# A two-layer decoder trunk on one core: the next stage's first weights split before the norm into x tiles, later weight work queued behind the norm, the convolution's third product on its own

## The chip, the core and the metric

The kernel runs on one core of one Trainium2 chip. The metric is the device time of one execution in microseconds (us); the time of a kernel is the median of its runs. Engines are called PE (TensorE; PEld its weight loads), DVE (VectorE), ACT (ScalarE), POOL (GpSimd) and SP (SyncE, which only issues DMAs here).

## What is computed

A residual stream of 16 learned meta tokens and 512 input tokens (528 columns), 1024 wide, goes through two layers. Layer 0 is FFN, short gated convolution, FFN; layer 1 is FFN, attention with a forget gate, FFN. Keys, values and gates are computed once between the layers. Everything is in float32.

```python
def swiglu(x, wg, wu, wd):
    return (jax.nn.silu(x @ wg) * (x @ wu)) @ wd

for l in range(DEPTH):                                   # 2
    h = layer_norm(ALPHA * h + 0.5 * swiglu(h, ffn1_wg[l], ffn1_wu[l], ffn1_wd[l]), ...)
    if l < N_A:                                          # layer 0
        mix = short_conv(h, conv_w_in[l], conv_w[l], conv_w_out[l])
    else:                                                # layer 1
        mix = forgetting_attention(h, attn_w_q[j], attn_w_o[j], k_sh, v_sh, c_sh)
    h = layer_norm(ALPHA * h + mix, ...)
    h = layer_norm(ALPHA * h + 0.5 * swiglu(h, ffn2_wg[l], ffn2_wu[l], ffn2_wd[l]), ...)
    if l == N_A - 1:
        k_sh, v_sh, c_sh = shared_kv(h, kv_w, f_bias)
```

`short_conv` projects to three parts (gate b, gate c, value), convolves c times value over three positions, and multiplies by b.

## The kernel before

**Layout.** The stream `y` lies transposed in SBUF: 128 partitions by 8 blocks of the 1024 channels by 528 columns. The columns are worked on in two halves, h = 0 and 1, of 264 columns in layer 0 and 256 in layer 1 (`SPAN`).

**Products.** Every float32 operand is split into a high part, rounded to a narrower format by a cast on ACT, and a low part, the rest, by a subtraction on DVE. A product is three matmuls for each step k: high times low, low times high, high times high (`gemms`, L229). For weights the split is `split_w` (cast L121 into `wh`, subtraction L122 into `wl`), for activations `split_x` (L242 into `xh`, L243 into `xl`). Weights come by DMA from SP into three `raw` buffers of 1 MB and are split into five pairs of tiles `wh`, `wl`; 14 x tiles (`xtile`) hold right operands. `gemms` counts a step (`tick`) after three matmuls; `later(n, fn)` traces `fn` n steps on, which puts `fn`'s matmuls there in PE's queue.

**Order.** The order on PE is that of the program (`manual_schedule`). On the other engines a scheduler orders the instructions when the kernel is built, by readiness in a model and by priority, which follows the program; a norm's operations get a priority 600 higher (`SOON`). Each queue then runs in its order.

**A Mixed stage** (two FFNs of layer 0, keys and values, both FFNs of layer 1) multiplies 256 gate columns and 256 up columns at a time as two-by-two blocks with seven products in place of eight (`Unit`: p1 to p7 with left operands a11, a12, s1 to s4, a22 and right operands b11, b21, t1 to t4, b22). The right operands t1 to t4 are sums of the halves of `y` and are made on DVE in `Mixed.sums`; the left sums s1 to s4 are made in `Quads.sums`. As t1 to t4 need both halves of the columns, the first 256 columns of most stages are a `Direct` unit: plain products, first for half 0 (b11, b21), then for half 1 (b12, b22), 96 matmuls each, with left operands a11, a21, a12, a22. Its a11 goes into x tiles (L557), the others into `wh`, `wl`.

**A boundary.** Five of the six norms sit in a `down` (L463): the product back to 1024 channels, in the order column blocks 0 to 2 of half 0, 0 to 2 of half 1, 3 to 7 of half 0, 3 to 7 of half 1. A product for one block and half is 18 matmuls (6 steps) at the end of an FFN and 24 (8 steps) after convolution or attention. Each block is added to `y` on DVE (L475), squared on ACT (L387) and summed on POOL (L391 `y`, L393 squares). `LAG` steps after the last block of a half, `Norm.post` (L395) puts eight statistics matmuls (L401) on PE. `Norm.finish` follows: v (L411 on ACT, L412 on DVE), eight small operations on DVE (L332 to L340), b (L416), then in pairs of blocks the scaling L420, L421 on DVE, L424 on ACT and `split_x`. Five such boundaries matter here: into the convolution (1), into the second FFN (2), into keys and values (3), into the queries (4) and into the last FFN (5). Boundaries 2, 3 and 5 lead to a `Direct` unit; 1 and 4 to plain products (`Plain`).

**Convolution and queries.** `conv_u` (L719) makes gate c and value (`pcc`, `pcv`) for a block and half, `conv_b` (L734) gate b (`pcb`); from block 2 on, L757 runs all three in lockstep. `project` (L894) runs several heads in lockstep: L1005 three heads of half 0.

Of the kernel before, what the change touches and what calls it, by code (L numbers as in the profile page):

```python
# [35 lines left out]
LAG = (5, 7)  # L36
# [10 lines left out]
def trunk_kernel(  # L47
# [60 lines left out]

    def split_w(src, shape, home=None):
# [12 lines left out]
        nc.vector.tensor_tensor(b, src, a.bitcast(F32), ALU.subtract)  # L122
# [34 lines left out]
    class Quads:  # L157
# [4 lines left out]
        def __init__(self, aps):  # L162
            self.aps, self.raws, self.got, self.home = aps, {}, {}, {}
# [15 lines left out]
        def sums(self):  # L179
            if "s" in self.got:  # L180
                return
            s = wp.tile([P, KD * P], F32, tag="ws", bufs=1, name="s")
            s = s.rearrange("p (j k n) -> p j k n", j=2, k=KH)
            self.got["s"] = s
            a11, a21, a22 = self.part(0, 0), self.part(1, 0), self.part(1, 1)
            nc.vector.tensor_tensor(s, a21, a22, ALU.add)  # L186
            nc.vector.tensor_tensor(a21, a11, a21, ALU.add)
            nc.vector.tensor_tensor(a11, a11, s, ALU.add)

        def __call__(self, name):  # L190
            if name not in self.got:
                if name[0] == "s":
                    self.sums()
                if name == "s4":
                    a12 = self.part(0, 1)
                    nc.vector.tensor_tensor(a12, a12, self.part(0, 0), ALU.add)
# [4 lines left out]
                self.got[name] = split_w(src, (2, KH, P), self.home.get(name))  # L201
# [39 lines left out]
    def split_x(dst_h, dst_l, src32):  # L241
        nc.scalar.copy(dst_h, src32)  # L242
        nc.vector.tensor_tensor(dst_l, src32, dst_h.bitcast(F32), ALU.subtract)  # L243


    class Plain:
# [6 lines left out]
        def made(self, h, m):  # L253
# [8 lines left out]
            split_x(a[:, k:k + 2, :w], b[:, k:k + 2, :w], yv[:, m:m + 2, :])  # L262
# [80 lines left out]
    class Norm:  # L343
# [63 lines left out]
        def finish(self, h, pd, pv):  # L407
# [10 lines left out]
            for m in range(0, KD, 2):  # L418
# [8 lines left out]
                self.to.made(h, m)  # L427
# [35 lines left out]
    def down(layer, w, kn, operands, first, norm, scale, opened=None):  # L463
# [8 lines left out]
        for (m, h), ps in products(seq, w, kn, operands, opened or {}, layer):  # L472
# [96 lines left out]

    def run_units(units, finish, direct=None, after=None):  # L570
# [26 lines left out]
    def ffn(layer, wg, wu, wd, ln, xs, to, last=None, ready=None, fresh=True):  # L597
# [3 lines left out]
        for c, (f0, fn) in enumerate(CHUNKS):  # L601
# [35 lines left out]
            run_units(units, finish, direct if fresh and c == 0 else None)  # L637
# [6 lines left out]
            if last and c == len(CHUNKS) - 1:  # L644
# [4 lines left out]
                 norm if c == len(CHUNKS) - 1 else None, 2 * ALPHA)  # L649
# [5 lines left out]
    first = Quads([a[0][:, :256] for a in (ffn1_wg, ffn1_wu)])  # L655
# [458 lines left out]
```

## Time and profile before

| | |
|---|---|
| median of 3 runs | 1980.35 us (1979.28 to 1980.63) |
| profiled execution | 1983.2 us |
| its span, first to last instruction | 1981.4 us |
| mean granted clock of PE | 0.980 |
| PE busy | 1891.8 us (95%) |
| DVE busy | 1405.8 us (71%) |
| ACT busy | 874.4 us (44%) |
| POOL busy | 135.0 us (7%) |
| chain that ended last | PE 90%, DVE 8%, ACT 1%, DMA 1% |

An engine's busy time is the time in which it executes an instruction. An instruction's idle time before it is put down to the instruction that released it last. The granted clock is the share of 2.4 GHz that PE was given; 0.50 is 1.2 GHz. In a row of a stretch the busy times stand in the order PE, PEld, DVE, ACT, POOL. In the rows, `pc<-xh,wl` is the tile written and the tiles read; names that share a helper are told apart by tile, as most matmuls stand on one line.

### The profile page before, as it was taken

What the parts mean: (1) busy time and instruction counts of PE and PEld (TensorE: products, weight loads), DVE (VectorE), ACT (ScalarE), POOL (GpSimd) and SP (SyncE); (2) the same over time, 40 slices, a digit from 0 to 9 for tenths busy, and PEclk for the clock granted to TensorE, in tenths of its full rate; (3) what the DMA queues carried; (4) which work ended last, traced back from release to release, by engine and by line L of the source; (5) the groups of instructions that cost most, each with busy time, mean ns of one, the idle gap of its engine ahead of it and who ended that gap; (6) DMA issues with size and microseconds to landing.
All of it is one profiled execution on the core that took longest, in us unless ns stands there. A gap on an engine that the chain in (4) does not pass through costs nothing.

```text
span 1981.4 us, 34598 instructions
## 1 busy us (share of the span) xinstructions
PE 1891.8 (95%) x14467; PEld 1830.8 (92%) x14467; DVE 1405.8 (71%) x2077; ACT 874.4 (44%) x1459; POOL 135.0 (7%) x198
## 2 busy tenths in 40 slices
PE   8999999899998999999699999999989979999997
PEld 7999999799997999999699999999978879989897
DVE  6676767754369776767788876767578687858685
ACT  5353535432235353535454544434455444535360
POOL 0000000400031000000411000000210210000000
PEclk9999999999998999999899999999999989999999
DMA  4332333212221332323223423232423203333341
GB/s 142 118 105 88 107 91 118 91 65 86 86 65 43 119 116 87 107 86 107 86 71 126 149 65 125 84 112 81 155 74 121 65 33 97 96 98 110 101 129 43
DMA packets 180682, 190.43 MB, mean 96 GB/s; under 512 B 5834, under 2 KB 174070, under 8 KB 180526
## 3 DMA queue, kind: packets, MB, share of 16 engines
q1 hardware_dynamic: 178510, 182.74, 28.9%
q0 software_dynamic: 2016, 5.49, 0.8%
q8 instruction: 113, 1.85, 0.4%
q14 instruction: 43, 0.35, 0.1%
HBM read 181.76 MB, written 6.44 MB: 95 GB/s over the span
## 4 chain that ended last, share of the span: by engine, by line
PE 90%; DVE 8%; ACT 1%; issue 1%; DMA 1%; SPq 0%; DVEq 0%; ACTq 0%
PE pb L229 26%; PE pc L229 17%; PE pa L229 6%; PE pq L229 2%; PE pcc L229 2%; PE pcb L229 2%; DVE wl L122 2%; PE pcv L229 2%; PE psc L919 1%; PE po L977 1%; DVE y L420 1%; DVE y L421 1%; DMA raw<-in_ffn_wg_dram 1%; DVE xl L243 1%; PE pd L401 1%
## 5 line engine op out<-in xcount | busy, mean ns | idle before, releaser
L122 DVE TENSOR_TENSOR wl<-raw,wh 128x1024 fp32r<-128x1024 f32 (+1 forms) x440 | 526.3, 1199 | 188.8 <-ACT wh L121 180.3
L121 ACT CAST wh<-raw 128x1024 fp32r<-128x1024 f32 (+1 forms) x440 | 438.9, 1003 | 466.7 <-PE pc L229 76.7
L229 PE MATMUL pb<-xh,wh 128*128 128x264 f32 (+1 forms) x1408 | 398.7, 283 | 0.0
L229 PE MATMUL pb<-xl,wh 128*128 128x264 f32 (+1 forms) x1408 | 397.8, 283 | 0.0
L229 PE MATMUL pb<-xh,wl 128*128 128x264 f32 (+1 forms) x1408 | 397.8, 283 | 0.0
L229 PE MATMUL pc<-xh,wl 128*128 128x264 f32 (+1 forms) x960 | 279.9, 292 | 42.6 <-DVE wl L122 39.3
L229 PE MATMUL pc<-xl,wh 128*128 128x264 f32 (+1 forms) x960 | 279.2, 291 | 3.1 <-DVE xl L243 3.1
L229 PE MATMUL pc<-xh,wh 128*128 128x264 f32 (+1 forms) x960 | 278.6, 290 | 0.0
L229 PEld LDWEIGHTS pb<-xh,wl 128*128 128x128 f32 x1408 | 264.6, 188 | 0.3
L229 PEld LDWEIGHTS pb<-xl,wh 128*128 128x128 f32 x1408 | 264.5, 188 | 0.3
L229 PEld LDWEIGHTS pb<-xh,wh 128*128 128x128 f32 x1408 | 264.5, 188 | 0.0
L229 PEld LDWEIGHTS pc<-xh,wl 128*128 128x128 f32 x960 | 187.5, 195 | 44.4 <-DVE wl L122 37.5
L229 PEld LDWEIGHTS pc<-xl,wh 128*128 128x128 f32 x960 | 187.5, 195 | 4.6 <-DVE xl L243 4.5
L229 PEld LDWEIGHTS pc<-xh,wh 128*128 128x128 f32 x960 | 187.6, 195 | 0.0
L229 PE MATMUL pa<-xh,wh 128*128 128x264 f32 (+1 forms) x352 | 99.7, 283 | 0.0
L229 PE MATMUL pa<-xh,wl 128*128 128x264 f32 (+1 forms) x352 | 99.5, 283 | 0.0
L229 PE MATMUL pa<-xl,wh 128*128 128x264 f32 (+1 forms) x352 | 99.5, 283 | 0.0
L186 DVE TENSOR_TENSOR s<-raw 128x1024 f32<-128x1024 f32 x44 | 53.7, 1220 | 18.0 <-DMA raw<-in_ffn_wu_dram 14.5
L121 ACT CAST wh<-s 128x1024 fp32r<-128x1024 f32 x44 | 46.0, 1046 | 46.2 <-PE pc L229 5.5
L229 PEld LDWEIGHTS pa<-xh,wl 128*128 128x128 f32 x352 | 66.2, 188 | 0.0
L229 PEld LDWEIGHTS pa<-xl,wh 128*128 128x128 f32 x352 | 66.1, 188 | 0.0
L229 PEld LDWEIGHTS pa<-xh,wh 128*128 128x128 f32 x352 | 66.1, 188 | 0.0
(1919 smaller groups left out, 4540.7 us busy)
## 6 DMA issues: line engine op xcount, KB each, us to landing
raw<-in_ffn_wg_dram SPq DMA_DIRECT2D x88, 512.0 KB, 3.9
raw<-in_ffn_wu_dram SPq DMA_DIRECT2D x88, 512.0 KB, 4.8
raw<-in_ffn_wd_dram SPq DMA_DIRECT2D x48, 768.0 KB, 4.5
raw<-in_conv_w_in_dram SPq DMA_DIRECT2D x12, 1024.0 KB, 4.9
raw<-in_ffn_wd_dram SPq DMA_DIRECT2D x16, 512.0 KB, 3.9
raw<-in_kv_w_dram SPq DMA_DIRECT2D x16, 512.0 KB, 4.8
raw<-in_conv_w_out_dram SPq DMA_DIRECT2D x4, 1024.0 KB, 5.4
raw<-in_attn_w_q_dram SPq DMA_DIRECT2D x4, 1024.0 KB, 5.9
```

What stands on the lines that cost most here:

```text
L121: nc.scalar.copy(a, src)
L122: nc.vector.tensor_tensor(b, src, a.bitcast(F32), ALU.subtract)
L186: nc.vector.tensor_tensor(s, a21, a22, ALU.add)
L229: nc.tensor.matmul(ps, lhsT=a[:, k, :], rhs=b(k), start=start and k == ks[0] and j == 0, stop=stop and k == ks[-1] and j == 2, skip_group_ ...
L243: nc.vector.tensor_tensor(dst_l, src32, dst_h.bitcast(F32), ALU.subtract)
L401: nc.tensor.matmul(ps, lhsT=ones_all, rhs=t, start=n == 0, stop=n == 1)
L420: nc.vector.tensor_tensor(ym, ym, rb, ALU.mult)
L421: nc.vector.tensor_tensor(ym, ym, bb, ALU.add)
L919: nc.tensor.matmul(ps, lhsT=q[:, M + t * P:M + (t + 1) * P], rhs=kt[:, a:b], start=True, stop=True)
L977: nc.tensor.matmul(po[:, q0:S], lhsT=vt[:, j * P:(j + 1) * P], rhs=pT[j // 2][:, j % 2, q0:S], start=j == 0, stop=False)
```

## The change

The first weights of a stage that follows a norm (four for a `Direct` unit, two for convolution and queries) are split inside the `down` before the norm, after its seventh product, into x tiles; just before them all of the `down`'s own weights are split, and all four of its loads are now traced at its head. `issue_after` gives an instruction a place behind another in the order of its engine: low halves and left sums that are traced after a norm's `finish` go behind that norm's last `split_x` on DVE. The next unit's a11 and a12 and its left sums are traced from inside `Mixed.sums` (`left`), between the right sums. `LAG` goes from (5, 7) to (4, 5). In the convolution `conv_u` and `conv_b` run one after the other.

```diff
-LAG = (5, 7)
+LAG = (4, 5)
...
+    newest = []
+
+    def behind():
+        return tc.issue_after(newest[-1].ins) if newest else nullcontext()
...
         nc.scalar.copy(a, src)
-        nc.vector.tensor_tensor(b, src, a.bitcast(F32), ALU.subtract)
+        with behind():
+            nc.vector.tensor_tensor(b, src, a.bitcast(F32), ALU.subtract)
...
-        def __init__(self, aps):
-            self.aps, self.raws, self.got, self.home = aps, {}, {}, {}
+        def __init__(self, aps, home=None):
+            self.aps, self.raws, self.got, self.home = aps, {}, {}, home
...
-            nc.vector.tensor_tensor(s, a21, a22, ALU.add)
-            nc.vector.tensor_tensor(a21, a11, a21, ALU.add)
-            nc.vector.tensor_tensor(a11, a11, s, ALU.add)
+            with behind():
+                nc.vector.tensor_tensor(s, a21, a22, ALU.add)
+                nc.vector.tensor_tensor(a21, a11, a21, ALU.add)
+                nc.vector.tensor_tensor(a11, a11, s, ALU.add)
...
-                    nc.vector.tensor_tensor(a12, a12, self.part(0, 0), ALU.add)
+                    with behind():
+                        nc.vector.tensor_tensor(a12, a12, self.part(0, 0), ALU.add)
...
-                self.got[name] = split_w(src, (2, KH, P), self.home.get(name))
+                self.got[name] = split_w(src, (2, KH, P), self.home)
...
             t = {}
+            self.left("a11")
+            self.left("a12")
             for k in range(0, KH, 2):
                 t1 = new("t1")
...
+            self.left("s1")
             for k in range(0, KH, 2):
                 t3, t2 = new("t3"), new("t2")
...
-                self.to.made(h, m)
+                last = self.to.made(h, m)
+            newest.append(last)
...
-    def down(layer, w, kn, operands, first, norm, scale, opened=None):
+    def down(layer, w, kn, operands, first, norm, scale, opened=None, ahead=None):
...
-        for (m, h), ps in products(seq, w, kn, operands, opened or {}, layer):
+        for m in range(KD):
+            w.load(m)
+        for n, ((m, h), ps) in enumerate(products(seq, w, kn, operands, opened or {}, layer)):
+            if ahead and n == 2 * LEAD:
+                for m_ in range(KD):
+                    w(m_)
+                ahead()
...
-            quads.home = {"a11": xtile}
...
+    def first_four(quads):
+        return lambda: [quads(n) for n in ("a11", "a21", "a12", "a22")]
+
     def run_units(units, finish, direct=None, after=None):
         if direct:
+            units[0].xs.left = units[1].quads
...
     turn_x(0)
+    first_four(first)()
     later(KD, lambda: turn_x(1))
...
-    ffn(0, ffn1_wg[0], ffn1_wu[0], ffn1_wd[0], 0, xs0, xc, ready=first)
-
     w_in = [Weights(conv_w_in[0], 0, KD, j * D, KD) for j in range(3)]
+    for j in (1, 2):
+        w_in[j].home = {0: xtile}
+    ffn(0, ffn1_wg[0], ffn1_wu[0], ffn1_wd[0], 0, xs0, xc, ready=first,
+        ahead=lambda: (w_in[1](0), w_in[2](0)))
...
-            run([conv_u(i, h), conv_b(i, h)])
+            run([conv_u(i, h)])
+            run([conv_b(i, h)])
...
+    f2 = Quads([a[0][:, :256] for a in (ffn2_wg, ffn2_wu)], xtile)
     down(0, Weights(conv_w_out[0], 0, KD, 0, KD), KD, z_operands, True,
-         Norm(0, 1, EPS, xs1), ALPHA)
+         Norm(0, 1, EPS, xs1), ALPHA, ahead=first_four(f2))
...
-    ffn(0, ffn2_wg[0], ffn2_wu[0], ffn2_wd[0], 2, xs1, xs2)
+    kv_quads = [
+        Quads([kv_w[:, j * D + i * 256:j * D + (i + 1) * 256] for j in range(2)], None if i else xtile)
+        for i in range(H // 2)]
+    ffn(0, ffn2_wg[0], ffn2_wu[0], ffn2_wd[0], 2, xs1, xs2, ready=f2, ahead=first_four(kv_quads[0]))
...
-    ffn(1, ffn1_wg[1], ffn1_wu[1], ffn1_wd[1], 3, xs2, xq, fresh=False)
+    q_w = Weights(attn_w_q[0], 0, KD, 0, H)
+    q_w.home = {m: xtile for m in range(2)}
+    ffn(1, ffn1_wg[1], ffn1_wu[1], ffn1_wd[1], 3, xs2, xq, ahead=lambda: (q_w(0), q_w(1)))
...
-    down(1, o_w, KD, o_operands, True, Norm(1, 4, EPS, xs3), ALPHA, opened)
+    f4 = Quads([a[1][:, :256] for a in (ffn2_wg, ffn2_wu)], xtile)
+    down(1, o_w, KD, o_operands, True, Norm(1, 4, EPS, xs3), ALPHA, opened, first_four(f4))
```

## Rows read from the trace of the kernel before

**Rows 1.** Waits of TensorE, whole span: total us, times, longest.

```profile
PE pc L229 <- DVE wl L122: 39.3, 5, 15.6
...
PE pcb L229 <- DVE wl L122: 6.3, 5, 1.3
```

**Rows 2.** Timeline, PE, boundary 4: start, us, what, [idle before, releaser].

```profile
1451.93 0.58 PE L229 MATMUL pq<-xh,wl 128*128 128x256 f32 x1 [8.39 <-ACT xh L242]
```

**Rows 3.** Stretches, all engines: length, busy us (x instructions), PEclk, DMA, GB/s.

```profile
380.00:400.00 20.00, 11.17 (x60) 10.19 (x59) 16.58 (x27) 9.64 (x18) 5.01 (x5) 0.74 0.32 106
592.00:632.00 40.00, 28.97 (x190) 27.78 (x189) 35.95 (x54) 20.90 (x39) 5.07 (x4) 0.79 0.13 40
968.00:996.00 28.00, 12.41 (x74) 11.80 (x73) 23.87 (x36) 10.60 (x19) 4.99 (x4) 0.70 0.24 75
1442.00:1462.00 20.00, 11.30 (x75) 10.59 (x75) 18.01 (x31) 9.52 (x18) 4.90 (x4) 0.83 0.31 105
1600.00:1640.00 40.00, 28.50 (x184) 27.33 (x183) 35.32 (x55) 19.80 (x37) 5.00 (x4) 0.79 0.12 40
640.00:660.00 20.00, 20.00 (x165) 19.83 (x164) 15.31 (x21) 9.94 (x15) 0.00 (x0) 1.00 0.73 238
430.00:540.00 110.00, 103.66 (x839) 102.61 (x838) 43.84 (x75) 29.65 (x51) 0.50 (x5) 1.00 0.29 96
```

**Rows 4.** Timeline, PE, boundary 2: first and last of four statistics pairs.

```profile
578.41 0.61 PE L401 MATMUL pd<-y,ones_all 128*128 128x264 f32 x2
...
579.74 0.61 PE L401 MATMUL pv<-s,ones_all 128*128 128x264 f32 x2
```

**Rows 5.** Timeline, DVE, boundary 3, first half: chain begins, a split, scaling.

```profile
960.80 0.43 DVE L412 SCALAR_TENSOR_TENSOR v<-pv,v 128x264 f32<-128x264 f32 x1 [3.26 <-PE pv L401]
...
962.62 1.77 DVE L122 TENSOR_TENSOR wl<-raw,wh 128x1024 fp32r<-128x1024 f32 x1
...
973.93 1.52 DVE L420 TENSOR_TENSOR y<-y,r 128x528 f32<-128x528 f32 x2
```

**Rows 6.** Timeline, DVE, boundary 3, second half: chain begins, scaling, first low half.

```profile
992.77 0.43 DVE L412 SCALAR_TENSOR_TENSOR v<-pv,v 128x264 f32<-128x264 f32 x1 [3.86 <-PE pv L401]
...
997.19 1.32 DVE L420 TENSOR_TENSOR y<-y,r 128x528 f32<-128x528 f32 x2
...
1001.52 0.70 DVE L243 TENSOR_TENSOR xl<-y,xh 128x528 fp32r<-128x528 f32 x1
```

**Rows 7.** Timeline, ACT, boundary 2: last two casts of the norm, then weights.

```profile
595.87 0.61 ACT L242 CAST xh<-y 128x528 fp32r<-128x528 f32 x1
...
597.22 0.61 ACT L242 CAST xh<-y 128x528 fp32r<-128x528 f32 x1
...
598.38 1.98 ACT L121 CAST wh<-raw 128x1024 fp32r<-128x1024 f32 x2
```

**Rows 8.** Timeline, SP, before boundary 2: first load of the next stage.

```profile
547.87 0.37 SPq L171 DMA_DIRECT2D raw<-in_ffn_wg_dram  x1
```

**Rows 9.** Timeline, DVE, boundary 4: chain, scaling, addition, a split, last split.

```profile
1434.76 0.42 DVE L412 SCALAR_TENSOR_TENSOR v<-pv,v 128x256 f32<-128x256 f32 x1 [3.15 <-PE pv L401]
...
1447.67 1.48 DVE L420 TENSOR_TENSOR y<-y,r 128x512 f32<-128x512 f32 x2
...
1453.28 0.41 DVE L475 TENSOR_TENSOR y<-y,pd__15665 128x256 f32<-128x256 f32 x1
...
1454.22 1.21 DVE L122 TENSOR_TENSOR wl<-raw,wh 128x1024 fp32r<-128x1024 f32 x1
...
1456.23 0.69 DVE L243 TENSOR_TENSOR xl<-y,xh 128x512 fp32r<-128x512 f32 x1 [0.20 <-ACT xh L242]
```

**Rows 10.** Timeline, ACT, boundary 4: square of the last column block.

```profile
1455.29 0.40 ACT L387 ACTIVATE sq<-y 128x256 f32<-128x256 f32 x1
```

**Rows 11.** Timeline, POOL, boundary 3: a sum alone, one beside a split.

```profile
957.30 0.76 POOL L393 TENSOR_TENSOR s<-s,sq 128x264 f32<-128x264 f32 x1
...
966.00 1.73 POOL L393 TENSOR_TENSOR s<-s,sq 128x264 f32<-128x264 f32 x1
```

More of the change, by code (lines that the diff above doesn't have):

```diff
@@ L1 @@
 import math
-from contextlib import ExitStack
+from contextlib import ExitStack, nullcontext
 import concourse.bass as bass
@@ L242, in split_x @@
         nc.scalar.copy(dst_h, src32)
-        nc.vector.tensor_tensor(dst_l, src32, dst_h.bitcast(F32), ALU.subtract)
+        return nc.vector.tensor_tensor(dst_l, src32, dst_h.bitcast(F32), ALU.subtract)
     class Plain:
@@ L261, in made @@
             k = m % KH
-            split_x(a[:, k:k + 2, :w], b[:, k:k + 2, :w], yv[:, m:m + 2, :])
+            return split_x(a[:, k:k + 2, :w], b[:, k:k + 2, :w], yv[:, m:m + 2, :])
         def sums(self):
@@ L296, in made @@
             i, k = m // KH, m % KH
-            split_x(*self.tiles(f"b{i + 1}{h + 1}", k), self.part(i, h, k))
+            return split_x(*self.tiles(f"b{i + 1}{h + 1}", k), self.part(i, h, k))
         def sums(self):
@@ L595, in run_units, with ffn @@
                 nxt.p2()
-    def ffn(layer, wg, wu, wd, ln, xs, to, last=None, ready=None, fresh=True):
+    def ffn(layer, wg, wu, wd, ln, xs, to, last=None, ready=None, ahead=None):
         norm = Norm(layer, ln, 4 * EPS, to) if not last else None
@@ L631, in ffn @@
                 c0 = (f0 + 2 * i) * P
-                q = ready if ready and not (c or i) else Quads([a[:, c0:c0 + 256] for a in (wg, wu)])
-                if c or i or not fresh:
+                fresh = ready and not (c or i)
+                q = ready if fresh else Quads([a[:, c0:c0 + 256] for a in (wg, wu)])
+                if not fresh:
                     units.append(Unit(q, xs, [lambda m: gtile("g"), lambda m: gtile("u")]))
@@ L636, in ffn @@
                     units.append(Direct(q, xs))
-            run_units(units, finish, direct if fresh and c == 0 else None)
+            run_units(units, finish, direct if ready and c == 0 else None)
             def operands(h, hh=hh, hl=hl):
@@ L648, in ffn @@
             down(layer, wts, fn, operands, c == 0,
-                 norm if c == len(CHUNKS) - 1 else None, 2 * ALPHA)
+                 norm if c == len(CHUNKS) - 1 else None, 2 * ALPHA, None,
+                 ahead if c == len(CHUNKS) - 1 else None)
     ctx.enter_context(tc.manual_schedule(engines={mybir.EngineType.PE}))
     xs0 = Mixed(0)
-    first = Quads([a[0][:, :256] for a in (ffn1_wg, ffn1_wu)])
+    first = Quads([a[0][:, :256] for a in (ffn1_wg, ffn1_wu)], xtile)
     half = D // 2
@@ L856, in trunk_kernel @@
     kv_units = []
-    for i in range(H // 2):
-        q = Quads([kv_w[:, j * D + i * 256:j * D + (i + 1) * 256] for j in range(2)])
+    for i, q in enumerate(kv_quads):
         kv_units.append(Unit(
@@ L874, in trunk_kernel @@
     xq = Plain(1)
-    ffn(1, ffn1_wg[1], ffn1_wu[1], ffn1_wd[1], 3, xs2, xq, fresh=False)
+    q_w = Weights(attn_w_q[0], 0, KD, 0, H)
+    q_w.home = {m: xtile for m in range(2)}
+    ffn(1, ffn1_wg[1], ffn1_wu[1], ffn1_wd[1], 3, xs2, xq, ahead=lambda: (q_w(0), q_w(1)))
     opened = {}
     o_w = Weights(attn_w_o[0], 0, KD, 0, KD)
-    q_w = Weights(attn_w_q[0], 0, KD, 0, H)
     qs, kts, vts, cks, ss, pTs, oh, ol = ({} for _ in range(8))
@@ L1079, in last @@
         flush()
-    ffn(1, ffn2_wg[1], ffn2_wu[1], ffn2_wd[1], 5, xs3, None, last=last)
+    ffn(1, ffn2_wg[1], ffn2_wu[1], ffn2_wd[1], 5, xs3, None, last=last, ready=f4)
 _INS = [
```

## Prediction

> **What bounds the kernel now.** TensorE. I read the list of its waits first, then busy time and granted clock by stretch, then each engine's rows around the waits. Between stages nothing waits: 165 matmuls in 20 us, 0.121 us each, at full clock [rows 3]. The waits sit in two places. One is five stage boundaries, where a norm's output becomes the next right operand: 1, the convolution (from 382 us); 2, the second FFN (593); 3, keys and values (970); 4, the queries (1443); 5, the last FFN (1602). Waits for the low half of a weight add up to 39.3 us [rows 1]; at 1 and 4 TensorE waits for the norm's own output, 8.4 us at 4 [rows 2]. The other place is the convolution's steady part: 6.3 us in five waits of `pcb` for a low half [rows 1].
>
> What a boundary loses in all is its stretch, less 0.121 us for each matmul and 1.9 us for the eight statistics matmuls among them (four pairs, 578.41 to 580.35 [rows 4]): 20 - 52 x 0.121 - 1.9 = 11.8 us at 1, 40 - 182 x 0.121 - 1.9 = 16.0 at 2, 18.1 at 3, 10.0 at 4, 16.8 at 5 [rows 3]. Sum 72.7 us. It holds some half clock (1.2 GHz): the granted clock of the five stretches is 0.70 to 0.83 [rows 3], and a boundary without waits would win that back too.
>
> Why TensorE waits. At boundary 3 the statistics of the first half of the columns arrive on DVE at 960.80 and the scaling (L420) begins at 973.93, 13.1 us later: four weight splits of 1.77 us are queued into the chain of small operations between [rows 5]. The same chain without splits, for the second half, takes from 992.77 to 997.19, 4.4 us [rows 6]. Boundaries 2, 3 and 5 have a second reason: the first split (a11) goes into an x tile, and at 2 its cast runs at 598.38, behind the norm's last cast at 597.22 [rows 7], although its weights were asked for at 547.87 [rows 8]. I read that as the x pool handing out tiles in program order: a11 stands behind the norm's tiles.
>
> **The change, part by part.** *Early splits into x tiles* (`ahead`). The next stage's first weights are split after the seventh product of the norm's `down`, and that `down`'s own weights just before them. No work is added: 16 splits (2, 4, 4, 2, 4) move forward with their casts on ACT; SP's loads keep their order. Both reasons go. The chain becomes 4.4 us [rows 6] plus two `y` additions of 0.4 [rows 9], 5.2 instead of 13.1, and LAG 4 for 5 starts it one step (three matmuls, 0.36 us) earlier.
>
> Boundary 3: L420 at 960.8 - 0.4 + 5.2 = 965.6. The first high half is usable 4.3 us after L420 (1447.67 to 1451.93 at boundary 4 [rows 2, 9]), the first low half 5.0 us after it [rows 6]. That is 969.9 and 970.6. The statistics end about when v begins, and `down` has 75 matmuls after them (one step of three, four products of 18), 9.1 us: it ends at 969.8. So 0.9 us of waiting, and 0.8 for the second pair, which ACT makes 1.4 us after the first [rows 7]. Boundary 1 has the same shape. At 2 and 5 a product of `down` has eight steps, so 105 matmuls (12.7 us) follow the statistics, and L420 comes 4 us earlier than now: TensorE finds everything ready.
>
> *A new wait, the second half's statistics.* LAG 5 for 7 puts them 1.8 us into the next stage. They need the last column block's addition, which DVE begins 5.6 us after L420 [rows 9], and its square, which ACT has done at 8.0 us [rows 10]; the last sum on POOL (0.76 to 1.73 us [rows 11]) ends by 9.5. At 1 and 3 TensorE gets there at 4.3 + 0.9 + 1.8 = 7.0. Cost 1 to 2.5 us, I take 2; the whole next stage is queued behind it on TensorE. The second half's norm then comes in time at 1, 3 and 4; at 2 and 5 it arrives together with TensorE and costs 0.9 us of pairs, at 3 the same.
>
> *Later weight work behind the norm* (`behind`). Low halves and sums traced after a norm go behind its last split on DVE. At boundary 4 this costs. Three heads advance in step (L896), and only heads 0 and 1 are split early. Head 2's low half has to follow the norm's last split, which ends 9.3 us after L420, and takes 1.2 itself: 10.5 [rows 9]. L420 will be at 1434.8 - 0.4 + 5.2 = 1439.6, the low half is there at 1450.1, and TensorE, which could begin at 1443.9, stops within its first step. Now it begins at 1451.9 [rows 2]. 5.5 us of waiting stay, and I take 2 us of half clock: 7.5 lost instead of 10.0. At 2, 3 and 5 two left operands of the next unit and three sums (6 us of DVE) come after the second norm instead of before it. DVE was busy 35.95 of 40 us in the stretch of boundary 2 [rows 3]. 4 us of the norm move out at its front and two splits of 1.77, which leaves 28.4 us of work for a stretch that shrinks to 28: the first mixed unit will wait for DVE. I take 3 us at 2 and 5 (0 to 7), 0 at 3, where the direct unit's output goes through ACT alone.
>
> *x tiles.* The eight homes and the norm's first six are all 14. t1 to t4 get their tiles as TensorE releases the homes in the second direct half, at 2.9, 5.8, 8.7 and 11.6 us of it; the first is wanted at 17.4. Cost 0, and 1 (0 to 2) at boundary 5, where four x tiles hold the attention's output until `down` ends. At the kernel's start the same move is taken at 0 (up to 5).
>
> *Splits beside POOL.* The moved splits run while POOL adds up the norm's sums. A sum beside a split takes 1.73 us instead of 0.76 [rows 11], a split 1.77 instead of 1.21 [rows 5, 9]. At 3 POOL is done at 958.06 [rows 11], 1 to 2 us before the statistics use it (they begin 2 us before v [rows 4, 5], at 958.8). Two new collisions eat that: 0.5 us at 1 and at 3, from 0 to 2.3. The Trainium skill, SBUF — State Buffer, Who interferes with whom, says that a DVE operation with two SBUF inputs and a GpSimd operation that reads SBUF exclude one another for a whole instruction. The rows agree (0.97 us more is most of a split). It speaks against moving splits here, and by it each of the 16 would hold up the sums; that is part of rival B.
>
> *The third product apart* (L756). `pcc` and `pcv` run first. `pcb`'s weights get a slot that comes free 2.9 us before the old block ends, and are wanted 5.8 us into the new one. All five waits go, 6.3 us (5 to 6.4) [rows 1]. What hides the splits is DVE's room: 43.84 of 110 us busy there [rows 3].
>
> *All four loads at the head of `down`*: the order in the pool is the same, 0. Some 3.6 us of the 39.3, at 1072 us in the keys and values, stay, give or take 4: DVE's order there is drawn anew.
>
> Sum of what is lost afterwards. 1: 0.9 + 0.8 + 2 + 0.5 and 1 of half clock = 5.2. 2: 0.9 + 3 = 3.9. 3: 0.9 + 0.8 + 2 + 0.9 + 0.5 and 3 of half clock = 8.1. 4: 7.5. 5: 0.9 + 3 + 1 = 4.9. Together 29.6 in place of 72.7: 43.1 us won, with 6.3 from the convolution 49.4. The profiled execution took 1983.2 us (span 1981.4), so 1933.8; the median of the runs is 1980.35, 2.9 less, which gives 1931.
>
> **Rivals.** A, less waiting than I charge: no stall at the statistics (4), DVE keeps up (6), the clock stays up (5): 15 us less, 1916. For it: each is a charge of 1 to 3 us that rests on the order DVE gets. Against it: the rows give each one a place.
>
> B, DVE or POOL becomes the bound: the first mixed units at 2, 3 and 5 lose 5 us more each, or the 16 collisions of 0.97 all count. 15 us more: 1946. For it: 28.4 us of work for 28. Against it: part of that work (t3, t4) is wanted late.
>
> C, the splits don't come early: DVE's order still puts them into the chain, and only the convolution's 6.3 us are won: 1974. Against it: the weights lie there 15 to 30 us before, and DVE has room.
>
> D, slower: the t tiles starve. If t1 to t4 are made only when the second direct half is over, DVE has to do before the third product two left halves, t1, three sums and s1 (6 x 1.21 + 4 x 0.70 = 10.1 us), before the fourth 5.4, then 2.6 and 4.0, and 16 x 0.42 = 6.7 for the direct outputs: 28.8 us against 17.5 for six products, and 3 us ahead of the first, as ACT stands at a cast without a tile. That is 14.3 us in each of four stages (the start too), 57 against 49.4 won: 1988. It decides from 12.4 us a stage. Against it: the homes come free one by one.
>
> **How the numbers follow.** Forecast 0.55, A 0.17, B 0.18, C 0.05, D 0.05. The forecast's bounds: half of A's 15 us below, 1923; above, half of statistics 1, units 8, collisions 3.6, boundary 5 1, keys and values 4, so 9: 1940. The range takes in A and B and stops short of C: 1910 to 1951. Within 0.2% (4 us, about what a measurement of this kernel can tell from no change) lies only what is between C and D: same 0.03, slower 0.05, faster 0.92.
>
> **What would show it.** L122 gone between L412 and L420 of the first half at all five boundaries (else C). No `pcb` wait. No wait at the first matmul of stages 2 and 5; at 4 one of some 5 us for `wl`. Waits of the statistics (L401) for ACT or POOL at 1 and 3, up to 2.5 us. Waits of `pb` or `pc` for DVE in the first mixed units up to 3 us (none: A; over 6: B or D). I am wrong if head 2 doesn't wait at boundary 4, or if DVE bounds the first mixed units for long.

## The result and the profile after

The changed kernel takes 1965.09 us (median of 4 runs, 1964.06 to 1967.33) beside 1980.49 us for the kernel before (median of 4): a ratio of 0.9923, 95% interval 0.9906 to 0.9940. The forecast of 1931 us was wrong, and the range from 1910 to 1951 does not hold the time. The change won 15 us, not 49. The profiled execution's span is 1963.6 us, 17.8 less than before. In the changed kernel the split is `split_w` L127 (cast) and L129 (subtraction), `split_x` L251 and L252, the matmuls L238, the statistics L414, v L425, the scaling L433 and L434.

First the waits of TensorE in the kernel after, whole span (total us, times, longest; they answer [rows 1, 2]):

```profile
PE pq L238 <- DVE wl L129: 12.9, 2, 7.9
PE pb L238 <- ACT sg L648: 11.0, 2, 6.3
PE pcc L238 <- DVE wl L129: 10.8, 1, 10.8
...
PE pc L238 <- DVE wl L129: 6.4, 2, 3.6
...
PE pc L374 <- ACT first L370: 3.3, 4, 2.3
...
PE pv L414 <- ACT sq L400: 2.2, 4, 0.8
PE pd L414 <- POOL s L404: 1.8, 3, 1.0
```

Of the old waits little is left: `pc` for low halves fell from 39.3 to 6.4 us (2.8 at the start and 3.6 in the keys and values), and `pcb` is absent. At 1 and 4 TensorE's wait for the norm's own output fell from 8.5 and 8.4 us to 1.1 each. Three new pairs stand in their place, 34.7 us together; none of the three was in the list before.

Then the five boundaries by stretch, and one stretch of stage 2 (length, busy us (x instructions) of PE, PEld, DVE, ACT, POOL, then PEclk, DMA share, GB/s; they answer [rows 3], moved to where each boundary now lies):

```profile
380.00:420.00 40.00, 26.04 (x174) 23.85 (x173) 27.55 (x46) 17.46 (x34) 4.23 (x6) 0.83 0.23 79
590.00:630.00 40.00, 33.47 (x242) 31.88 (x241) 35.41 (x59) 20.86 (x42) 4.99 (x6) 0.91 0.00 1
960.00:988.00 28.00, 24.09 (x180) 22.30 (x179) 25.50 (x44) 16.06 (x34) 4.09 (x4) 1.00 0.01 1
1420.00:1460.00 40.00, 25.42 (x162) 23.76 (x162) 24.25 (x39) 16.03 (x34) 4.16 (x7) 0.74 0.16 53
1588.00:1628.00 40.00, 31.79 (x238) 30.48 (x237) 36.32 (x62) 22.14 (x44) 5.45 (x6) 0.92 0.00 1
596.00:626.00 30.00, 24.49 (x190) 24.07 (x189) 29.51 (x48) 15.49 (x29) 0.00 (x0) 0.93 0.00 1
```

By the prediction's own measure (stretch, less 0.121 us for each matmul and 1.9 us for the eight of the statistics) stage 1 loses 40 - 166 x 0.121 - 1.9 = 18.0 us, stage 2 9.8, stage 3 5.3, stage 4 19.5, stage 5 10.3. A second measure, used for every kernel below: take the same matmul, by its place in PE's order, in two traces, and see how its lead over the kernel before changes from one side of a stage to the other.

| stage | lost before | forecast lost after | lost after | forecast won | won, by the same matmul |
|---|---|---|---|---|---|
| 1 convolution begins | 11.8 | 5.2 | 18.0 | 6.6 | -6.0 |
| 2 second FFN | 16.0 | 3.9 | 9.8 | 12.1 | 6.4 |
| 3 keys and values | 18.1 | 8.1 | 5.3 | 10.0 | 13.4 |
| 4 queries | 10.0 | 7.5 | 19.5 | 2.5 | -9.9 |
| 5 last FFN | 16.8 | 4.9 | 10.3 | 11.9 | 6.1 |
| sum | 72.7 | 29.6 | 62.9 | 43.1 | 10.0 |
| convolution, steady | | | | 6.3 | 7.9 |

10.0 and 7.9 are the whole difference of the spans; the rest of the kernel adds up to nothing (-3.5 around the `first` matmul ahead of stage 4, +2.9 in the keys and values and the FFN after them, +0.8 at the start and in the second FFN). So the question is why stages 1 and 4, where 9 us were expected, lost 16, and why 2 and 5 gave half.

**Stage 3: the mechanism works.** DVE in the kernel after, first half's chain (it answers [rows 5]; start, us, instruction):

```profile
952.62 0.43 DVE L425 SCALAR_TENSOR_TENSOR v<-pv,v 128x264 f32<-128x264 f32 x1 [4.18 <-PE pv L414]
...
954.10 0.88 DVE L348 SCALAR_TENSOR_TENSOR a<-a,v 128x264 f32<-128x264 f32 x1
...
958.79 1.42 DVE L433 TENSOR_TENSOR y<-y,r 128x528 f32<-128x528 f32 x2
```

From v to the scaling it takes 6.2 us, not 13.1; no split lies between. Forecast was 5.2. Most of the extra 1 us is three small operations that ran beside sums on POOL and took 0.87 to 0.88 us instead of 0.43.

**Stages 1 and 4: low halves behind the wrong norm.** PE, four of the new waits and the one at `first` (the rows at 623.41, of stage 2, and 1391.60 are for later); the last bracket is the idle time before the row and what ended it:

```profile
404.28 0.59 PE L238 MATMUL pcc<-xh,wl 128*128 128x264 f32 x1 [10.77 <-DVE wl L129]
...
623.41 0.59 PE L238 MATMUL pb<-xh,wl 128*128 128x264 f32 x1 [4.75 <-ACT sg L648]
...
1391.60 0.39 PE L374 MATMUL pc<-first,ones_pre 128*128 128x256 f32 x1 [2.34 <-ACT first L370]
...
1429.91 0.58 PE L238 MATMUL pq<-xh,wl 128*128 128x256 f32 x1 [4.98 <-DVE wl L129]
...
1449.50 0.58 PE L238 MATMUL pq<-xh,wl 128*128 128x256 f32 x1 [7.91 <-DVE wl L129]
```

And DVE at the same times, stage 1 first, then stage 4:

```profile
389.60 0.43 DVE L425 SCALAR_TENSOR_TENSOR v<-pv,v 128x264 f32<-128x264 f32 x1 [1.55 <-PE pv L414]
...
402.38 0.71 DVE L252 TENSOR_TENSOR xl<-y,xh 128x528 fp32r<-128x528 f32 x1 [0.47 <-ACT xh L251]
403.01 2.35 DVE L129 TENSOR_TENSOR wl<-raw,wh 128x1024 fp32r<-128x1024 f32 x2
...
1428.12 1.74 DVE L129 TENSOR_TENSOR wl<-raw,wh 128x1024 fp32r<-128x1024 f32 x1
1434.94 0.42 DVE L425 SCALAR_TENSOR_TENSOR v<-pv,v 128x256 f32<-128x256 f32 x1 [5.09 <-PE pv L414]
...
1447.62 0.69 DVE L252 TENSOR_TENSOR xl<-y,xh 128x512 fp32r<-128x512 f32 x1 [0.58 <-ACT xh L251]
1448.23 3.49 DVE L129 TENSOR_TENSOR wl<-raw,wh 128x1024 fp32r<-128x1024 f32 x3
```

The convolution's order is block 0, then block 1, both on the first half's columns, and only then the second half. Block 1's weights are split when they are first named. By then the second half's norm has been traced, so `behind()` queues them behind it: 13.4 us of norm (389.60 to 403.01) stand before low halves that a product of the *first* half wants at 393.5 (the row at 404.28, less its 10.77 us of idle time). Before, the same low halves lay in the first half's chain, in front. At stage 4 it happens in two steps. Head 2's low half waits for the first norm (4.98 us, as forecast). PE's order puts the second half's statistics behind that product, so DVE sits idle for 5.09 us and the second norm starts that much later; heads 3 and 4, still on the first half, have their low halves behind that second norm: 7.91 us more.

**Stages 2 and 5: the first mixed unit waits for a bank.** ACT in the kernel after:

```profile
622.44 0.63 ACT L251 CAST xh<-t 128x528 fp32r<-128x528 f32 x1 [0.42 <-DVE t L332]
622.98 0.94 ACT L648 ACTIVATE sg<-pc 128x264 f32<-128x264 f32 x3
```

`pb` takes the PSUM banks of the direct unit's first half. They are freed by its gate (`sg`, L648, which reads them). The gate could have run when its products ended, by 606.8 us, but stands on ACT behind casts of t tiles, and these wait for DVE. DVE was busy 29.51 of the 30 us from 596 to 626 (the last row of the stretches). It stood idle just before that, for the second half's statistics:

```profile
596.18 0.43 DVE L425 SCALAR_TENSOR_TENSOR v<-pv,v 128x264 f32<-128x264 f32 x1 [3.48 <-PE pv L414]
```

Whether the bank is the cause or only the last link is what four of the experiments ask.

### The profile page after: what moved, and what is told of

Its sections match the earlier page's. It is cut to its first block, busy times and chain, and to the rows that moved or that the text cites. A ratio compares the mean times of both kernels' runs of the same rounds, so it can differ in the third digit from the quotient of the medians.

```text
span 1963.6 us, 34602 instructions
## 1 busy us (share of the span) xinstructions
PE 1886.4 (96%) x14467; PEld 1822.4 (93%) x14467; DVE 1401.3 (71%) x2077; ACT 876.1 (45%) x1459; POOL 133.6 (7%) x198
## 4 chain that ended last, share of the span: by engine, by line
PE 86%; DVE 9%; ACT 2%; issue 1%; DMA 1%; POOL 1%; SPq 0%; DVEq 0%; ACTq 0%; POOLq 0%
PE pb L238 26%; PE pc L238 15%; PE pa L238 6%; PE pcv L238 2%; PE pcc L238 2%; PE pcb L238 2%; PE pq L238 2%; DVE wl L129 1%; DVE xl L252 1%; DVE y L433 1%; DVE y L434 1%; PE psc L953 1%; PE po L1011 1%; ACT y L437 1%; PE pt L708 0%
## 5 line engine op out<-in xcount | busy, mean ns | idle before, releaser
L129 DVE TENSOR_TENSOR wl<-raw,wh 128x1024 fp32r<-128x1024 f32 (+1 forms) x440 | 518.8, 1185 | 201.2 <-ACT wh L127 187.1
L127 ACT CAST wh<-raw 128x1024 fp32r<-128x1024 f32 (+1 forms) x440 | 439.2, 1003 | 480.9 <-PE pc L238 74.0
L238 PE MATMUL pb<-xh,wl 128*128 128x264 f32 (+1 forms) x1408 | 400.8, 285 | 11.0 <-ACT sg L648 11.0
L238 PE MATMUL pb<-xh,wh 128*128 128x264 f32 (+1 forms) x1408 | 400.2, 284 | 0.0
L238 PE MATMUL pb<-xl,wh 128*128 128x264 f32 (+1 forms) x1408 | 400.0, 284 | 0.0
L238 PE MATMUL pc<-xh,wl 128*128 128x264 f32 (+1 forms) x960 | 273.8, 285 | 7.4 <-DVE wl L129 6.4
L238 PEld LDWEIGHTS pb<-xh,wl 128*128 128x128 f32 x1408 | 266.9, 190 | 11.8 <-ACT sg L648 11.4
L238 PE MATMUL pc<-xl,wh 128*128 128x264 f32 (+1 forms) x960 | 272.9, 284 | 3.4 <-DVE xl L252 3.4
L238 PE MATMUL pc<-xh,wh 128*128 128x264 f32 (+1 forms) x960 | 272.4, 284 | 0.0
L238 PEld LDWEIGHTS pb<-xh,wh 128*128 128x128 f32 x1408 | 267.8, 190 | 0.0
L238 PEld LDWEIGHTS pb<-xl,wh 128*128 128x128 f32 x1408 | 266.9, 190 | 0.3
L238 PEld LDWEIGHTS pc<-xh,wl 128*128 128x128 f32 x960 | 181.4, 189 | 8.4 <-DVE wl L129 3.9
L238 PEld LDWEIGHTS pc<-xl,wh 128*128 128x128 f32 x960 | 181.5, 189 | 4.5 <-DVE xl L252 4.5
L238 PEld LDWEIGHTS pc<-xh,wh 128*128 128x128 f32 x960 | 181.8, 189 | 0.0
L238 PE MATMUL pa<-xh,wl 128*128 128x264 f32 (+1 forms) x352 | 99.7, 283 | 0.0
L238 PE MATMUL pa<-xh,wh 128*128 128x264 f32 (+1 forms) x352 | 99.6, 283 | 0.0
L238 PE MATMUL pa<-xl,wh 128*128 128x264 f32 (+1 forms) x352 | 99.5, 283 | 0.0
L127 ACT CAST wh<-s 128x1024 fp32r<-128x1024 f32 x44 | 46.1, 1047 | 48.4 <-DVE s L194 7.9
L238 PEld LDWEIGHTS pa<-xh,wh 128*128 128x128 f32 x352 | 66.3, 188 | 0.0
L238 PEld LDWEIGHTS pa<-xh,wl 128*128 128x128 f32 x352 | 66.2, 188 | 0.0
L238 PEld LDWEIGHTS pa<-xl,wh 128*128 128x128 f32 x352 | 66.2, 188 | 0.0
L437 ACT ACTIVATE y<-y,vecs 128x264 f32<-128x264 f32 (+1 forms) x80 | 43.9, 597 | 45.1 <-DVE y L434 45.1
```

The source lines that it names most:

```text
L127: nc.scalar.copy(a, src)
L238: nc.tensor.matmul(ps, lhsT=a[:, k, :], rhs=b(k), start=start and k == ks[0] and j == 0, stop=stop and k == ks[-1] and j == 2, skip_group_ ...
L437: nc.scalar.activation(yv[:, j, :], yv[:, j, :], AF.Identity, scale=vecs[:, c:c + 1], bias=vecs[:, 48 + c:49 + c])
```

## Experiments

All times are medians with the kernel before run beside them on the same chip (1979.4 to 1980.6 us); ratios are to that.

**e1, one part alone: the third product apart.** Done on the kernel before.

```
-            run([conv_u(i, h), conv_b(i, h)])
+            run([conv_u(i, h)])
+            run([conv_b(i, h)])
```

> The kernel before with one part of the change: the convolution's third product is run behind the other two instead of beside them. The record counted five waits of 1.27 us for pcb, 6.3 us in all: 1974.0. What the two traces show when the same matmul is compared in both: the lead of the kernel after grows by 1.66 us in each of the five columns, since a wait ends a run of matmuls that overlap by 0.16 us: 8.3 us, 1972. Rival: the third product waits for its bank wherever it stands: 1980.

Measured: 1971.79 us, ratio 0.9960 (0.9946 to 0.9974), 7.6 us won. The stretch of 100 us that held the five waits (columns as above):

```profile
430.00:530.00 100.00, 100.00 (x826) 100.00 (x824) 42.79 (x72) 28.98 (x50) 0.40 (x4) 1.00 0.31 102
```

PE has no gap left. The gain is 1.66 us for a column by the same matmul, so it is more than the waits' 1.27: a wait also ends a run of overlapping matmuls. In the kernel before, the product that waited at 450.63 us started 1.55 us after the one ahead of it, where 0.121 us lie between two in a run. Half of the whole change's gain is this one line.

**e2, the queueing taken away.** Done on the kernel after.

```
     def behind():
-        return tc.issue_after(newest[-1].ins) if newest else nullcontext()
+        return nullcontext()
```

> The kernel after without the queueing behind the norm: low halves of weights and left sums go where the scheduler puts them; the early splits stay. Theory 1 (the queueing holds the second products at stages 1 and 4 but clears the chain of the norm at all five): stages 1 and 4 lose their waits of 10.8, 5.0 and 7.9 us and get low halves inside the first half's chain again (three of 1.2 to 1.8 us and as many stretched steps, some 7 us each), stages 2, 3 and 5 get such intrusions of 5 to 8 us too: 1965 - 24 + 14 + 18 = some 1973, 1965 to 1980. Theory 2 (the early splits bring the gain and the queueing only costs): the waits go and nothing comes back: 1940. Theory 3 (neither matters, the DVE's work as a whole sets the boundary): 1965.

Measured: 1957.34 us, ratio 0.9889 (0.9874 to 0.9904). The queueing costs 8 us in all, which none of the three theories gives, so it has to be read by stage (table below). At stage 3 the intrusions are back, and 13.7 us with them; DVE:

```profile
945.77 0.43 DVE L425 SCALAR_TENSOR_TENSOR v<-pv,v 128x264 f32<-128x264 f32 x1 [4.13 <-PE pv L414]
...
948.18 1.77 DVE L129 TENSOR_TENSOR wl<-raw,wh 128x1024 fp32r<-128x1024 f32 x1
...
950.90 1.78 DVE L129 TENSOR_TENSOR wl<-raw,wh 128x1024 fp32r<-128x1024 f32 x1
...
954.20 1.78 DVE L196 TENSOR_TENSOR raw<-raw,s 128x1024 f32<-128x1024 f32 x1
...
957.46 2.35 DVE L433 TENSOR_TENSOR y<-y,r 128x528 f32<-128x528 f32 x2
```

11.7 us from v to the scaling. At stages 1 and 4 the waits of 10.8, 5.0 and 7.9 us go and waits of 7.4 and 7.3 us for the norm come back, 8.3 and 10.4 us better than with the queueing; at stages 2 and 5 it decides little.

**e3, whole weights behind the first half's norm only.** The low halves of convolution, queries and `down` queue behind the last split of half 0; those of the mixed units stay behind the newest norm.

```
-    newest = []
+    newest, firsts = [], []
...
-    def behind():
+    def behind(of=newest):
-        return tc.issue_after(newest[-1].ins) if newest else nullcontext()
+        return tc.issue_after(of[-1].ins) if of else nullcontext()
...
-    def split_w(src, shape, home=None):
+    def split_w(src, shape, home=None, of=firsts):
...
-        with behind():
+        with behind(of):
...
-                self.got[name] = split_w(src, (2, KH, P), self.home)
+                self.got[name] = split_w(src, (2, KH, P), self.home, newest)
...
-            newest.append(last)
+            (newest if h else firsts).append(last)
```

> The kernel after, where only low halves of whole weights (convolution, queries, down) queue differently: behind the first half's norm, not behind the newest one; the low halves and sums of the mixed units stay behind the newest. Theory 1 (at stage 1 the 10.8 us and at stage 4 the 7.9 us are the second half's norm ahead of low halves that the first half's products need): at stage 1 five low halves (6.1 us) now stand ahead of the second norm's chain, the wait of 10.8 us and its 13.7 us at half clock go, 2 to 4 us come back before the second half's first product; at stage 4 the 7.9 us go, the 5.0 us stay; together 15 to 22 us: 1943 to 1950. Theory 2 (the low halves are late because DVE has no room whatever their order): the waits only change their names: 1960 to 1967. Theory 3 (the low halves ahead delay the second half's chain by as much as was won): 1958 to 1965.

Measured: 1943.34 us, ratio 0.9814 (0.9799 to 0.9829), 22 us under the changed kernel, as theory 1 has it. DVE at stage 1:

```profile
387.07 2.90 DVE L129 TENSOR_TENSOR wl<-raw,wh 128x1024 fp32r<-128x1024 f32 x2
389.89 0.42 DVE L425 SCALAR_TENSOR_TENSOR v<-pv,v 128x264 f32<-128x264 f32 x1
390.24 1.21 DVE L129 TENSOR_TENSOR wl<-raw,wh 128x1024 fp32r<-128x1024 f32 x1
...
399.65 1.32 DVE L433 TENSOR_TENSOR y<-y,r 128x528 f32<-128x528 f32 x2
```

Two low halves are ready before the second norm begins, mostly made in the time in which DVE had nothing to do. At stage 4 one wait is left of two, head 2's:

```profile
PE pq L238 <- DVE wl L129: 5.5, 1, 5.5
```

The second norm's scaling comes 5.6 us later than in the kernel after (399.65 for 394.02), and the price of that is 0.9 and 0.5 us at the second half's first product. By the same matmul stage 1 gives 10.1 of the 22 us and stage 4 10.8; some 3 more lie at the `first` matmul ahead of stage 4 (see the loads, below), and stage 3 gives 1 back.

**e5, the third head split early, too.** On the kernel of e3; q_w(2) also joins the early splits.

```
-    q_w.home = {m: xtile for m in range(2)}
+    q_w.home = {m: xtile for m in range(3)}
```

> The kernel of e3, where the early split at stage 4 takes the third head's weights too, into two more x tiles. Theory 1 (the wait of 5.5 us at the first column of stage 4 is head 2's low half behind the first half's norm, and the second half's statistics stand behind that wait on PE): the wait goes with its 6.8 us at half clock, the second norm starts 5 us earlier, nothing comes back: 1943 - 8 = 1934 to 1937. Theory 2 (fourteen x tiles are taken then, and the queries' own tiles wait for the last of FFN 1): a wait for xh takes its place: 1941 to 1948.

Measured: 1939.63 us, ratio 0.9789 (0.9773 to 0.9805), between the two theories' ranges; 4 us under e3 by the medians, with intervals that just overlap, and 4.0 at stage 4 by the same matmul (0.9 to 4.9). The 5.5 us wait is gone and no wait for a tile came. So theory 1's mechanism is there, and the gain is below its 6 to 9: the second half's statistics, now earlier, stall for 1.1 us for a square.

**e10, without the early splits of stages 1 and 4.** On the kernel of e3.

```
-    ffn(0, ffn1_wg[0], ffn1_wu[0], ffn1_wd[0], 0, xs0, xc, ready=first,
-        ahead=lambda: (w_in[1](0), w_in[2](0)))
+    ffn(0, ffn1_wg[0], ffn1_wu[0], ffn1_wd[0], 0, xs0, xc, ready=first)
...
-    ffn(1, ffn1_wg[1], ffn1_wu[1], ffn1_wd[1], 3, xs2, xq, ahead=lambda: (q_w(0), q_w(1)))
+    ffn(1, ffn1_wg[1], ffn1_wu[1], ffn1_wd[1], 3, xs2, xq)
```

> The kernel of e3 without the early splits of stages 1 and 4: the convolution's and the queries' first weights are split where they are first used, behind the first half's norm. Theory 1 (early splits and the place in DVE's queue are two halves of one gain): the first product of stage 1 waits for low halves behind the first norm, some 8 us in place of 1.1; at stage 4 one wait of some 9 us takes the place of 1.1 and 5.5; with some 10 us more at half clock: 1943 + 10 to 15 = 1953 to 1958. Theory 2 (the place in the queue is all): 1943.

Measured: 1954.09 us, ratio 0.9870 (0.9853 to 0.9886), 11 us above e3: theory 1. The waits of PE, first from 375 to 410 us, then from 1400 to 1460:

```profile
PE pcc L238 <- DVE wl L129: 9.6, 1, 9.6
...
PE pq L238 <- DVE wl L129: 10.7, 2, 9.4
```

Stages 1 to 5 so far, won over the kernel before by the same matmul:

| | 1 | 2 | 3 | 4 | 5 |
|---|---|---|---|---|---|
| after | -6.0 | 6.4 | 13.4 | -9.9 | 6.1 |
| e2: early, no queueing | 2.3 | 8.2 | -0.3 | 0.5 | 6.6 |
| e3: early, whole weights behind half 0 | 4.1 | 7.2 | 12.3 | 0.9 | 6.0 |
| e5: e3, third head early | 3.1 | 5.8 | 13.4 | 4.9 | 5.7 |
| e10: e3, stages 1 and 4 not early | -0.8 | 6.1 | 13.3 | -2.3 | 6.7 |

Stage 5 of e2 takes in 2.6 us that it lost just ahead of the stage. One stage differs by up to 2 us between kernels in which nothing of it was changed; smaller differences in a column mean nothing.

**e4, a higher priority for the gate.** In the kernel after, `sg` and its multiplication (L648, L649) were traced with the norm's priority.

```
+                with tc.high_priority(offset=SOON):
-                nc.scalar.activation(sg, pg, AF.Silu)
-                nc.vector.tensor_tensor(sg, sg, pu, ALU.mult)
+                    nc.scalar.activation(sg, pg, AF.Silu)
+                    nc.vector.tensor_tensor(sg, sg, pu, ALU.mult)
```

> The kernel after, where only the first unit's gate (its ACT and DVE steps, which free the banks of its products) gets the priority that the norm has. Theory 1 (at stages 2 and 5 the 4.8 and 6.3 us are banks held because the gate stands behind the casts of the sums on ACT, though its products are done some 15 us earlier): both waits and their 6.8 us at half clock go, about 1 us comes back for s2's low half: 1965 - 18 + 2 = 1949 to 1953. Theory 2 (DVE's work between the norm and the first mixed unit is the bound, the bank only its last link): the wait moves to low halves or t tiles in the next products: 1962 to 1966. Theory 3 (the gate's DVE steps go into the second half's norm): slower, 1966 to 1970.

Measured: 1965.28 us, ratio 0.9928 (0.9913 to 0.9943), the same as the kernel after. ACT shows why this says nothing for either theory: the gate did not move, it is still behind the casts of t.

```profile
622.60 0.63 ACT L251 CAST xh<-t 128x528 fp32r<-128x528 f32 x1 [0.42 <-DVE t L332]
623.14 1.22 ACT L649 ACTIVATE sg<-pc 128x264 f32<-128x264 f32 x4
```

**e6, the gate moved for certain.** On the kernel of e3, `Mixed.sums` is cut in two; s1 and t2 to t4 are traced after the first direct half and queue behind its multiplication on DVE.

```
             for h in range(2):
                 units[0].half(h, direct)
+                if h == 0:
+                    with tc.issue_after(sgs[-1].ins):
+                        units[0].xs.rest()
```

> The kernel of e3, where the sums of the mixed units are traced in two parts: t1 and the low halves of a11 and a12 as before, the rest (s1, t2, t3, t4) behind the gate of the first half's direct products, so that this gate stands ahead of their casts on ACT. Theory 1 (the waits of 4.8 and 6.3 us are banks that the gate frees too late, because it stands behind casts whose inputs DVE makes late): both go, with 3.4 to 6.8 us each at half clock, and up to 2 us come back at s2's low half: 1943 - 14 = 1928 to 1933. Theory 2 (DVE's work between the norm and the first mixed unit is what binds; it was at work without a gap from 596 to 630 us in the kernel after): the waits move to s1, s2 or t2 with the same sum: 1940 to 1944.

Measured: 1940.26 us, ratio 0.9793 (0.9778 to 0.9808): 3 us under e3 by the medians, with intervals that overlap, and the lower end of theory 2's range. The gate now runs at 595.52, among the norm's last rows on ACT:

```profile
595.52 0.37 ACT L655 ACTIVATE sg<-pc 128x264 f32<-128x264 f32 x1
```

The stretch from 585 to 615, columns as above:

```profile
585.00:615.00 30.00, 27.48 (x220) 27.05 (x220) 29.75 (x47) 17.16 (x30) 0.00 (x0) 0.98 0.00 1
```

And what PE waits for from 590 to 660:

```profile
PE pc L238 <- ACT sg L655: 1.8, 1, 1.8
```

Both waits of `pb` are gone. PE now waits for the second half's gate, 1.8 us here and 3.5 at stage 5, and stages 2 and 5 win only 1.8 and 2.5 us more than in e3, about what unchanged stages differ by. DVE is busy 29.75 of 30 us.

**e8 and e9, both edits, and the sums in three parts.** e8 is e5 with e6. e9 puts t3's halves and t4 behind the second gate as well:

```
+            self.rest = lambda: self.last(t, new)
+
+        def last(self, t, new):
+            b = self.part
...
-                if h == 0:
-                    with tc.issue_after(sgs[-1].ins):
-                        units[0].xs.rest()
+                with tc.issue_after(sgs[-1].ins):
+                    units[0].xs.rest()
```

> The edits of e5 and e6 together on the kernel of e3. If both waits are what the two theories 1 say, the gains add, since they lie in different stages: 1920 to 1927. If DVE is what binds at stages 2 and 5: 1932 to 1938.

> The kernel of e8, with the sums in three parts: t3's halves and t4 behind the gate of the second half's direct products, too. In e8 the waits for pb turned into waits of 1.8 and 3.5 us for the next pair of banks, which the second half's gate frees. Theory 1 (a gate behind casts on ACT, again): these go with their half clock: 1937 - 6 = 1930 to 1933. Theory 2 (DVE's work is what binds, whatever is put first): the waits pass to t3, t4 or low halves: 1936 to 1941.

Measured: e8 1937.45 us, ratio 0.9778 (0.9764 to 0.9793), which is DVE's case; e9 1935.11 us, ratio 0.9772 (0.9757 to 0.9786), between the two theories' ranges and not to be told from e8. In e9 the waits of stage 2 (570 to 650) are spread over four links:

```profile
PE pb L238 <- ACT g L546: 1.5, 1, 1.5
PE pd__7131 L238 <- ACT hh L251: 1.0, 1, 1.0
PE pd__7131 L238 <- DVE hl L252: 1.0, 1, 1.0
PE pc L238 <- DVE xl L252: 0.7, 1, 0.7
```

DVE is full, in the stretch from 596 to 626:

```profile
596.00:626.00 30.00, 27.65 (x222) 27.07 (x222) 29.95 (x44) 18.68 (x34) 0.00 (x0) 1.00 0.11 34
```

By the same matmul e9 leads by 13.3 us more at the first mixed unit of stage 2 than ahead of the stage, and by 7.4 us more one chunk on, where e3 leads by 7.2: there the wait is passed along, not removed. At stage 5 e9 wins 9.8 us where e3 wins 6.0, so there order alone did give something. That DVE's work is the bound fits stage 2 best, but it is not shown: no kernel here gave DVE less to do. Nor did one use the 3.5 us for which DVE stands idle ahead of its full stretch (3.48 us before v at stage 2 of e9, as in the kernel after). e9 is by its median the fastest kernel here, 1.5% under the changed one and 2.3% under the one before.

**e7, the lags undone.** In the kernel after:

```
-LAG = (4, 5)
+LAG = (5, 7)
```

> The kernel after with the lags of the statistics as before, 5 and 7 steps in place of 4 and 5. Theory 1 (earlier statistics make PE stand 1.0 to 2.0 us at four of the stages for sums and squares, and start the second half's norm 0.7 us earlier where that norm is late): the stalls of some 6 us in all go, and the waits behind the second norm at stages 1, 2, 4 and 5 grow by up to 0.7 us each: 1961 to 1965. Theory 2 (the lags cause the new waits at stages 1 and 4): these shrink: below 1958.

Measured: 1968.24 us, ratio 0.9936 (0.9922 to 0.9951): 3 us slower by the medians, with intervals that overlap. The spans differ by 3.4 us (1967.0 and 1963.6). Fewer stalls at the statistics (2.2 us in place of 5.8 in the lists of waits) and longer waits behind the norms: `pcc` 11.7 for 10.8, `pq` 14.1 for 12.9, and the first high half at stages 1, 3 and 4 comes 0.7 us later each (1.8, 1.7 and 1.8 us of waiting for 1.1, 1.0 and 1.1). So theory 1's two terms are there, with the second larger than it said; theory 2 falls.

## Why the prediction was wrong

- *The chain without splits, 5.2 us*: right; 6.2 measured at stage 3. The splits left it at all five boundaries, so C falls.
- *Stage 3, 8.1 us lost*: 5.3. The pairs (1.0, 0.5, 0.6, 0.8) and the statistics are there as priced; the 3 us of half clock never came (1.00).
- *Stage 1, 5.2 us lost*: 18.0. **This is a failed step.** Under `behind` I named whose low halves are traced after which norm only for head 2 and the mixed units. I did not walk through the convolution's list of products, in which block 1 on half 0 comes before half 1. 10.8 us, and half clock after it (0.83 in the stretch). e3 shows it: it changes nothing but behind which norm whole weights stand, and the stage gets 10.1 us back.
- *Stage 4, 7.5 us lost*: 19.5. The wait for head 2, 5.5 forecast, was 5.0 (e5 takes it away). "The second half's norm then comes in time at 1, 3 and 4" is the **same failed step** again: I asked when the norm's output is wanted, not what is queued behind the norm. Heads 3 and 4 were, 7.9 us, and the norm itself started late because its statistics stand on PE behind head 2.
- *Stages 2 and 5, 3.9 and 4.9 us lost*: 9.8 and 10.3. DVE was as full as forecast (29.51 of 30 us) and the wait came at the unit forecast, but its last link is a bank that a gate on ACT frees late, which I had not named. The term was mis-sized: 3 us became 4.8 and 6.3; to them come about 1 us of statistics at each, which I had counted for 1 and 3 alone, and half clock (0.91 and 0.92), for which I had put nothing. That is the place that rival B names, in two of its three stages; whether DVE is the cause stays open.
- *Third product, 6.3*: 7.6 to 8.4. *x tiles, 0*: right, with no wait for a tile, and D falls. *Keys and values' 3.6 us stay*: right.
- *Loads at the head of `down`, 0*: nearly. Ahead of stage 4 a cast of the queries' weights waited on ACT for its load, and DVE's subtraction for that cast; the addition that `first` needs is queued behind. DVE in the kernel after:

```profile
1389.55 1.23 DVE L129 TENSOR_TENSOR wl<-raw,wh 128x1024 fp32r<-128x1024 f32 x1 [5.30 <-ACT wh L127]
1390.69 0.41 DVE L499 TENSOR_TENSOR y<-y,pd__15218 128x256 f32<-128x256 f32 x1
```

It cost 3.5 us here and 2.5 in e7, and under 1 in the other kernels with the same splits, whose casts waited 2.6 to 3.2 us for that load in place of 5.0 and 4.8. So the early split made an early addition wait for a DMA, which I had put at nothing.

The range was too narrow for a plain reason: its rivals priced terms that I had, and the loss came from a queue that I had walked only in part. 12.8 + 12.0 of the 33 us that the five stages fell short lie in the two stages of that one step, 5.9 + 5.4 the mis-sized one; stage 3 gave 2.8 back. The Trainium skill, PSUM — Partial Sum Buffer, Engine vs sequencer instructions, says that the queues of ScalarE, VectorE and GpSimdE are strict FIFO. Stage 1 agrees: two low halves whose casts had ended by 378.1 us waited until 403.01 behind a norm that they did not need. The last of these casts, on ACT:

```profile
377.02 1.06 ACT L127 CAST wh<-raw 128x1024 fp32r<-128x1024 f32 x1
```

What stays open: what binds at stages 2 and 5, and whether they can be had by giving DVE less to do or by an earlier second norm. Every order tried there kept DVE nearly full (29.51 to 29.95 of 30 us in the stretches shown), and none took work off it.

## What to carry to other kernels

An order "behind X" has to be checked for every instruction that it catches, by who wants its result first: list the consumers in the order of the engine that waits, and compare with where X stands. "The newest" at the time of tracing was not what the first consumer at stages 1 and 4 could afford. When a wait for a bank or a cast ends on an engine that waits for another, look whether that other is full: then moving the link may do little more than rename the wait, as at stage 2.

## What the runs showed of the hardware

The granted clock fell after long waits. In the stretch of stage 3, where the longest wait was 1.0 us, TensorE kept its full clock (1.00 in the kernel after, 0.70 before [rows 3]). In the stretches with waits of 4.8 to 10.8 us it was 0.74 to 0.92, so that a part of each ran at the lower of its two levels, 1.2 GHz: at stage 1 matmuls started 0.121 us apart before the wait of 10.8 us and 0.22 us apart after it, until 409.8 us. After a wait of 1.8 us it went either way. e6 and e8 both have that wait in stage 2, in the stretch from 596 to 626, and the granted clock there is 0.94 in e6 and 1.00 in e8. What makes the difference no run here shows.

Small DVE operations took twice as long beside POOL, not only large ones. L348, in the norm's own chain, took 0.88 us at 954.10 (stage 3), beside a sum on POOL, and 0.43 at stage 2 without one:

```profile
953.80 0.89 POOL L404 TENSOR_TENSOR s<-s,y 128x264 f32<-128x264 f32 x1 [2.25 <-DVE y L495]
...
578.86 0.43 DVE L348 SCALAR_TENSOR_TENSOR a<-a,v 128x264 f32<-128x264 f32 x1
```

The Trainium skill, SBUF — State Buffer, Who interferes with whom, states that DVE and GpSimd share one pair of ports under an exclusive lock; the forecast had charged that to the splits, and here the chain paid.
